# Dense products of a two-layer retention and RWKV-7 trunk: three products of 16-bit halves against one product of unsplit 32-bit floats

## The chip, the cores and the metric

The kernel runs on one core of one Trainium2 chip. The metric is the device time of one execution in microseconds (us). Engines are named as in the profile: PE is TensorE's matmul stream, PEld its weight loads, DVE is VectorE, ACT is ScalarE, POOL is GpSimd, SP is the queue from which the kernel issues its DMAs.

## The reference, cut to what matters

Two layers work on 1,024 latent tokens and 256 context tokens, 1,024 channels wide, all in 32-bit floats. Each layer normalises and modulates its input, sends it through one input projection, feeds two groups of heads (chunked retention, and an RWKV-7 delta-rule scan with a low-rank path for decay and learning rate), gates both, and adds an output projection to the residual:

```python
hl = rms_norm(xl, norm_w[layer]) * (1.0 + sc_l[:, None]) + sh_l[:, None]
pl = hl @ w_in[layer]                                   # 1024 -> 4*512 + 1664 + 512 columns
ql, kl, vl, gr_l, rw_l, gw_l = jnp.split(pl, IN_SPLITS, axis=-1)
...
w_log = -jax.nn.softplus(-(w0[d] + jnp.tanh(xw) @ w2[d])) - 0.5
a = jax.nn.sigmoid(a0[d] + xa @ a2[d])                  # the LoRA products
bonus = jnp.sum(hs(r) * hs(k) * r_k, axis=-1, keepdims=True) * hs(v)
```

The output projection is `mix @ w_out[layer]`, where mix holds the gated outputs of both groups (1,024 channels).

## The kernel before, in words

All 1,280 tokens (10 tiles of 128) lie along the free axis, channels on the partitions. A dense product has a 128x128 block of weights as its stationary operand and 256, 258 or 512 tokens as its moving operand; eight K tiles are summed in one PSUM bank.

**The dense products.** The helper `w_block` (L313) loads a column block of weights as 32-bit floats, two K tiles to a DMA, into `wraw` (3 buffers), and `w_split` (L308) makes two 16-bit halves of it: ACT writes the rounded half `whi` scaled by 16 (L309), ACT scales the raw block in place (L310), and POOL subtracts (L311) to give `wlo`. The normalised input is split likewise in `norm_chunk` (L332): `h_hi` by ACT, `h_lo` by DVE or POOL (L349 to L356). `project_steps` (L465) then issues three 16-bit products for each K tile, hi by hi, hi by lo and lo by hi (L477 to L479). The output projection does the same in `out_sum` (L799, products L804 to L806) with the halves of the mixed channels that `mix_in` (L785) makes. The LoRA stage `zstage` (L687) reads its input back from HBM twice over (tile `lap`), splits it and its weights, and multiplies in two 16-bit passes (L707). The sums over heads for the bonus (`head_sums`, L718) take two passes of the type float32r, of a rounded half and of its rest.

**The scan.** `prep` and `prep2` (L893, L934) prepare a step of 128 tokens in both directions, with a chain of small products, DVE masks and transposes and ACT copies; `seq` (L1031) carries the state through it. There are 40 steps in a layer, 10 for each of four pairs of heads. Their products are 32-bit and small (64 or 128 columns) or 16-bit (L980 to L1026).

**The order.** The dense work is a generator that yields its cost in units of microseconds; `pump` (L1199) draws from it a quota for each scan step (`QUOTA`, 15 in layer 0, 12 to 13 in layer 1), so that projections stand between the links of the scan on PE's queue. The scan is issued at high priority. When all dense work of a layer has been drawn, `out_last` (L852) adds the last two blocks of the output projection, normalises, and in the last layer writes the result. A projection yields `24 * (m1 - m0) / 2400`.

Of the kernel before, what the change touches and what calls it, by code (L numbers as in the profile page):

```python
# [11 lines left out]
F32R = mybir.dt.float32r  # L12
# [7 lines left out]
D = 1024  # L20
# [12 lines left out]
WS = 16.0  # L33
# [11 lines left out]
WB = 2  # L45
RAMP = 5.0
# [8 lines left out]
RB = 3  # L55
WMB = 3
XTB = 4
RETW = 32
NTM = (5, 7)
XB = 4  # L60
QUOTA = ((15.0, 15.0), (12.0, 13.0))
# [60 lines left out]
def hybrid_kernel(ctx: ExitStack, tc: tile.TileContext, a: dict, out: bass.AP, dbg: dict | None = None):  # L122
# [57 lines left out]
    bones32 = ln_pool.tile([128, 128], F32, name="bones32")  # L180
    load(bones32, a["c_bo"])
# [12 lines left out]
    bones = const.tile([128, 128], F32R, name="bones")  # L194
    nc.vector.tensor_copy(bones, bones32)
    bones2 = const.tile([128, 2], F32, name="bones2")
    nc.vector.tensor_copy(bones2, bones32[:, 0:128:64])
# [33 lines left out]
    la_d = dscr([2, 128, TOK], "la")  # L231
# [76 lines left out]
    def w_split(hi, lo, raw):  # L308
        nc.scalar.activation(hi, raw, AF.Copy, scale=WS)  # L309
        nc.scalar.activation(raw, raw, AF.Copy, scale=WS)  # L310
        nc.gpsimd.tensor_tensor(lo, raw, hi, ALU.subtract)  # L311

    def w_block(src, c0, rows=tuple(range(8))):  # L313
        halves = []
        for r0 in range(0, len(rows), 4):
            hi = wp.tile([128, 4, 128], F16, tag="whi", name="whi", bufs=WB)
            lo = wp.tile([128, 4, 128], F16, tag="wlo", name="wlo", bufs=WB)
            for q in range(r0, min(r0 + 4, len(rows)), 2):
                ks = slice(q - r0, q - r0 + 2)
                raw = wp.tile([128, 2, 128], F32, tag="wraw", name="wraw", bufs=RB)  # L320
                b0, b1 = rows[q:q + 2]
                cols = src[128 * b0:128 * b1 + 128, c0:c0 + 128].rearrange("(k p) n -> p k n", p=128)
                load(raw, cols[:, 0:b1 - b0 + 1:b1 - b0])
                w_split(hi[:, ks], lo[:, ks], raw)
            halves.append((hi, lo))
        return halves
# [5 lines left out]
    def norm_chunk(pool, l, h, mod, tiles, rs, get):  # L332
# [7 lines left out]
        for k in range(8):  # L340
            tm = pool.tile([128, 512], F32, tag="ntm", name="ntm", bufs=NTM[l])
            A, sh = mod["A"][:, c, k:k + 1], mod["B"][:, c, k:k + 1]
            by_pool = k % 4 == 1
            if by_pool:
                nc.gpsimd.tensor_tensor(tm[:, 0:n], get(k), rsb[:, 0:n], ALU.mult)
                nc.gpsimd.tensor_scalar(tm[:, 0:n], tm[:, 0:n], A, sh, ALU.mult, ALU.add)
            else:
                nc.vector.scalar_tensor_tensor(tm[:, 0:n], get(k), A, rsb[:, 0:n], ALU.mult, ALU.mult)
            for o, t0, m in _runs(tiles):  # L349
                hi, lo, t = h[0][:, k, t0:t0 + m], h[1][:, k, t0:t0 + m], tm[:, o:o + m]  # L350
                if by_pool:
                    nc.scalar.copy(hi, t)
                    nc.gpsimd.tensor_tensor(lo, t, hi, ALU.subtract)
# [11 lines left out]
    for l in range(DEPTH):  # L365
# [20 lines left out]
        nc.vector.tensor_scalar(hprm[:, 20:24], prm[:, R_RET:R_RET + 4], 0.5 / WS ** 2, None, ALU.mult)  # L386
# [32 lines left out]
        h = (hp.tile([128, 8, TOK], F16, name="h_hi"), hp.tile([128, 8, TOK], F16, name="h_lo"))  # L419
        h_hi, h_lo = h  # L420
# [44 lines left out]
        def project_steps(c0, pieces, sink):  # L465
            halves = w_block(w_in, c0)
            for piece in pieces:
# [4 lines left out]
                for hf in range(2):  # L472
                    hi, lo = halves[hf]
                    for k in range(4):
                        kk = 4 * hf + k
                        first, stop = kk == 0, kk == 7
                        nc.tensor.matmul(p[:, 0:n], hi[:, k, :], h_hi[:, kk, m0:m1], start=first, stop=False)  # L477
                        nc.tensor.matmul(p[:, 0:n], hi[:, k, :], h_lo[:, kk, m0:m1], start=False, stop=False)  # L478
                        nc.tensor.matmul(p[:, 0:n], lo[:, k, :], h_hi[:, kk, m0:m1], start=False, stop=stop)  # L479
                sink(p, m0, t0, t1)  # L480
                yield 24 * (m1 - m0) / 2400

        def conv(dst, p, m0, t0, t1, b):
# [5 lines left out]
            nc.scalar.activation(c[:, a0:a0 + w], p[:, o - 1 + a0:o - 1 + a0 + w], AF.Copy, scale=1.0 / WS)  # L489
# [28 lines left out]
        def ret_keys(rp, c):  # L518
# [3 lines left out]
            def sink(p, m0, t0, t1):  # L522
                nc.scalar.activation(kt[:, t0:t1], p[:, 0:t1 - t0], AF.Copy, scale=0.125 / WS)
                rope(kt[:, t0:t1], t0, t1)
# [3 lines left out]
        def ret_states(rp, c):  # L528
# [4 lines left out]
            def qsink(p, m0, t0, t1):  # L533
                nc.scalar.activation(qt[:, t0:t1], p[:, 0:t1 - t0], AF.Copy, scale=1.0 / WS)
                rope(qt[:, t0:t1], t0, t1)

            def vsink(p, m0, t0, t1):
                vch = [t256("vch") for _ in range(0, t1 - t0, 256)]
                for u, x in enumerate(vch):
                    nc.scalar.activation(x, p[:, 256 * u:256 * u + 256], AF.Copy, scale=1.0 / WS)  # L540
# [55 lines left out]
            yield from merge(own_states(), 4.3, queries(), 26)  # L596
# [69 lines left out]
        def gate_of(p):  # L666
            th = t256("gth")
            nc.scalar.activation(th, p[:, 0:256], AF.Tanh, scale=0.5 / WS)
# [4 lines left out]
        def lora():  # L673
            def sink(p, m0, t0, t1):
                la = t256("la")
                conv(la, p, m0, t0, t1, 12)
                nc.scalar.activation(la[0:64], la[0:64], AF.Tanh)
                for i in range(2):
                    for q in range(2):
                        load(la_d[i, 64 * q:64 * q + 64, t0:t1], la[64 * i:64 * i + 64])  # L680
# [6 lines left out]
        def zstage(p):  # L687

            raw = tz("wz")
            for i in range(2):  # L690
                src = a["rwkv_a2" if i else "rwkv_w2"][l][:, :, 128 * p:128 * p + 128].rearrange("d k n -> k d n")
                for q in range(2):
                    load(raw[64 * q:64 * q + 64, i].rearrange("k (d n) -> k d n", d=2), src)
            wz = pre.tile([128, 2, 256], F16, tag="wz", name="wz")
            nc.scalar.activation(wz, raw, AF.Copy, scale=WS)
            nc.vector.scalar_tensor_tensor(wz[64:128], raw[64:128], WS, wz[64:128], ALU.mult, ALU.subtract)
            for t0, t1, _, _ in CONV:
                la = tz("lap")
                load(la, la_d[:, :, t0:t1].rearrange("i p t -> p i t"))
                for i in range(2):  # L700
                    lh, ll = [pre.tile([128, 256], F16, tag="lr", name=nm, bufs=4) for nm in ("lh", "ll")]
                    nc.scalar.copy(lh, la[:, i])
                    nc.vector.tensor_tensor(ll, la[:, i], lh, ALU.subtract)
                    pz = pj("pz")
                    for d in range(2):
                        for q, lq in enumerate((lh, ll)):
                            nc.tensor.matmul(pz[:, 256 * d:256 * d + 256], wz[:, i, 128 * d:128 * d + 128], lq,  # L707
                                             start=(q == 0), stop=(q == 1))
                    th = tz("zth")
                    for d in range(2):  # L710
                        nc.scalar.activation(th[:, d], pz[:, 256 * d:256 * d + 256], AF.Tanh,
                                             bias=(ha0 if i else hw0)(d, p), scale=0.5 / WS)
# [4 lines left out]

        def head_sums(dst, x):  # L718

            xh, xl = [pre.tile([128, 256], F32R, tag="tr", name=nm, bufs=4) for nm in ("xh", "xlo")]  # L720
            nc.scalar.copy(xh, x)
            nc.gpsimd.tensor_tensor(xl, x, xh.bitcast(F32), ALU.subtract)
            nc.tensor.matmul(dst, bones, xh, start=True, stop=False)
            nc.tensor.matmul(dst, bones, xl, start=False, stop=True)

        def features(p):
# [29 lines left out]
            def vsink(pp, m0, t0, t1):  # L756
# [10 lines left out]
                head_sums(pp[:, 256:512], kt[:, t0:t1])  # L767
# [6 lines left out]
            yield from (rp if p else merge(zstage(p), 4.3, rp, 13))  # L774
# [10 lines left out]
        def mix_in(pool, tiles, b, key, bufs):  # L785
            n = 128 * len(tiles)
            mh = pool.tile([128, n], F16, tag=f"mh{key}", name="mh", bufs=bufs)
            ml = pool.tile([128, n], F16, tag=f"ml{key}", name="ml", bufs=bufs)
            for u in range(0, len(tiles), 2):
                raw = pre.tile([128, 2, 256], F32, tag="tz", name="mraw", bufs=TZB)[:, 0]  # L790
                for o, t0, m in _runs(tiles[u:u + 2]):
                    load(raw[:, o:o + m], mix_d[b][:, t0:t0 + m])
                piece = slice(128 * u, 128 * u + 256)
# [3 lines left out]
            return mh, ml  # L797

        def out_sum(x, tiles, k, parts):  # L799
# [3 lines left out]
            for i, ((hi, lo), (mh, ml)) in enumerate(parts):  # L803
                nc.tensor.matmul(p, hi, mh, start=(i == 0), stop=False)  # L804
                nc.tensor.matmul(p, hi, ml, start=False, stop=False)
                nc.tensor.matmul(p, lo, mh, start=False, stop=(i == len(parts) - 1))  # L806
            nc.vector.scalar_tensor_tensor(x, p, gmod[:, c, k:k + 1], x, ALU.mult, ALU.add)

        def out_part(chunks, key, stay):
# [6 lines left out]
            for k in range(8):  # L816
                halves = w_block(a["w_out"][l], 128 * k, EARLY)
                if stay:
                    out_last_weights(k)
                w = [[t[:, i % 4, :] for t in halves[i // 4]] for i in range(len(EARLY))]  # L820
                w += [[t[:, i, 128 * k:128 * k + 128] for t in ws] for i in range(len(LATE))]
                for tiles, ms in zip(chunks, mix):
# [10 lines left out]
                    yield 3 * len(ms) * 128 * len(tiles) / 2400  # L833
# [460 lines left out]
```

## Time and profile before

| | before |
|---|---|
| median of 3 runs | 2540.67 us (2540.04 to 2550.09) |
| the profiled execution | 2541.74 us |
| its span, first to last instruction | 2540.0 us |
| mean granted clock of PE in it | 0.945 of full speed |
| PE busy | 2332.3 us (92%) in 25223 instructions |
| DVE, ACT, POOL busy | 2016.9, 1209.1, 1017.3 us |
| moved by DMA | 302.82 MB, mean 119 GB/s |

Busy time counts every stretch in which an instruction of the engine is under way. Consecutive matmuls overlap in the records, since each record runs to the end of its drain; so the time from one start to the next, and not the duration, is what a product costs in a stream.

### The profile page before, as it was taken

How to read it: one execution, taken by the hardware profiler on the slowest of the kernel's cores; microseconds unless marked ns; L12 is line 12 of the kernel's file. 1: busy time of each engine (PE TensorE's matmuls, PEld its weight loads, DVE VectorE, ACT ScalarE, POOL GpSimd, SP SyncE). 2: the span in 40 equal slices, each digit the busy share in tenths (PEclk: the TensorE clock that was granted, in tenths of full speed). 3: DMA queues.
4: the chain of work that ended last, by engine and by line, in shares of the span. 5: the costliest groups of instructions: out<-in, count | busy, mean ns of one | idle time of the engine just before them, and what ended most of it. 6: DMA issues, size and time to landing. Idle time of an engine off the chain costs nothing. (4 is left out here: it accounts for less than half of the span.)

```text
span 2540.0 us, 68274 instructions
## 1 busy us (share of the span) xinstructions
PE 2332.3 (92%) x25223; PEld 1750.5 (69%) x25223; DVE 2016.9 (79%) x5822; ACT 1209.1 (48%) x3621; POOL 1017.3 (40%) x1511
## 2 busy tenths in 40 slices
PE   5789999999999999999986898999999999998997
PEld 2367767886787676777655677678768767676754
DVE  2658987998888787898657688889979988779866
ACT  4454554455455443345446545545645544334443
POOL 1444443344433433344425344444443444343442
PEclk8889999999999999799988899999999999987998
DMA  8754342444333432235433543434434433323444
GB/s 315 278 173 109 103 117 78 112 110 121 80 111 107 111 86 74 75 107 162 139 120 94 153 115 101 111 97 121 118 93 109 116 109 86 88 73 102 128 132 130
DMA packets 540013, 302.82 MB, mean 119 GB/s; under 512 B 239026, under 2 KB 526880, under 8 KB 537632
## 3 DMA queue, kind: packets, MB, share of 16 engines
q1 hardware_dynamic: 539680, 298.46, 41.0%
q8 instruction: 199, 3.26, 0.5%
q14 instruction: 134, 1.10, 0.1%
HBM read 212.21 MB, written 86.11 MB: 117 GB/s over the span
## 5 line engine op out<-in xcount | busy, mean ns | idle before, releaser
L477 PE MATMUL pproj<-h_hi,whi 128*128 128x256 f16 (+2 forms) x2128 | 632.2, 299 | 8.3 <-ACT h_hi L355 2.8
L478 PE MATMUL pproj<-h_lo,whi 128*128 128x256 f16 (+2 forms) x2128 | 632.3, 298 | 8.1 <-DVE h_lo L356 6.9
L479 PE MATMUL pproj<-h_hi,wlo 128*128 128x256 f16 (+2 forms) x2128 | 630.5, 298 | 4.5 <-POOL wlo L311 4.4
L311 POOL TENSOR_TENSOR wlo<-wraw,whi 128x256 f16<-128x256 f32 x360 | 252.2, 713 | 275.8 <-ACT wraw L310 230.9
L479 PEld LDWEIGHTS <-wlo 128*128 128x128 f16 x2128 | 214.0, 101 | 84.1 <-issue 13.1
L477 PEld LDWEIGHTS <-whi 128*128 128x128 f16 x2128 | 214.4, 101 | 74.3 <-issue 10.9
L478 PEld LDWEIGHTS <-whi 128*128 128x128 f16 x2128 | 213.3, 100 | 75.7 <-issue 16.1
L973 DVE STREAM_TRANSPOSE ttb<-tz 64x256 f16<-64x256 f16 x480 | 208.7, 435 | 29.2 <-ACT tz L994 24.4
L994 ACT CAST tz<-pinv 128x256 f16<-128x256 f32 x400 | 144.5, 370 | 178.1 <-PE pinv L993 161.6
L946 PE MATMUL pm<-own,bk 64*128 64x128 f32 (+1 forms) x1280 | 211.7, 300 | 9.5 <-DVE gq L949 4.6
L309 ACT ACTIVATE whi<-wraw 128x256 f16<-128x256 f32 x360 | 138.4, 412 | 153.9 <-DMA wraw<-in_w_in_dram 51.0
L963 POOL TENSOR_TENSOR il<-gq,c_id 64x256 f32<-64x256 f32 x160 | 122.9, 768 | 201.4 <-DVE gq L949 194.2
L946 PEld LDWEIGHTS pm<-own,bk 64*128 64x128 f32 x1280 | 168.9, 197 | 36.0 <-issue 10.9
L991 DVE TENSOR_TENSOR xx<-pinv,lvm 128x256 f16<-128x256 f32 x400 | 163.2, 416 | 36.0 <-PE pinv L980 32.7
L1049 PE MATMUL pseq<-st,own 64*64 64x64 f32 x2432 | 154.7, 231 | 0.0
L964 POOL TENSOR_TENSOR lo<-il,hi 64x256 f16<-64x256 f32 x160 | 116.9, 731 | 86.5 <-DVE hi L959 71.4
L310 ACT ACTIVATE wraw<-wraw 128x256 f32<-128x256 f32 x376 | 144.8, 410 | 4.4 <-ACT sbp L584 0.3
L980 PEld LDWEIGHTS <-hi 128*128 128x128 f16 x1920 | 105.1, 100 | 44.6 <-issue 17.3
L949 DVE TENSOR_TENSOR gq<-pm,c_m 128x256 f32<-128x256 f32 (+1 forms) x320 | 115.3, 400 | 25.0 <-PE pm L946 24.2
L1063 POOL TENSOR_TENSOR sf<-st,f 128x128 f32<-128x128 f32 x152 | 66.4, 437 | 164.7 <-DVE st L1081 147.9
L993 PE MATMUL pinv<-xx,ttb 128*128 128x64 f16 x1600 | 113.7, 196 | 16.6 <-DVE xx L991 15.4
L980 PE MATMUL pinv<-tz,hi 128*128 128x64 f16 x1600 | 115.6, 197 | 12.2 <-DVE tz L983 6.0
(250 smaller groups left out, 5648.9 us busy)
## 6 DMA issues: line engine op xcount, KB each, us to landing
ft<-feat SPq DMA_DIRECT2D x320, 160.0 KB
wraw<-in_w_in_dram SPq DMA_DIRECT2D x264, 128.0 KB
feat<-zth SPq DMA_DIRECT2D x80, 256.0 KB
wm<-in_w_mod_dram SPq DMA_DIRECT2D x16, 1024.0 KB
wraw<-in_w_out_dram SPq DMA_DIRECT2D x112, 128.0 KB
lap<-la SPq DMA_DIRECT2D x40, 256.0 KB
uv<-vt SPq DMA_DIRECT2D x320, 32.0 KB
wm<-in_w_mod_dram SPq DMA_DIRECT2D x16, 512.0 KB
```

What stands on the lines that cost most here:

```text
L309: nc.scalar.activation(hi, raw, AF.Copy, scale=WS)
L310: nc.scalar.activation(raw, raw, AF.Copy, scale=WS)
L311: nc.gpsimd.tensor_tensor(lo, raw, hi, ALU.subtract)
L477: nc.tensor.matmul(p[:, 0:n], hi[:, k, :], h_hi[:, kk, m0:m1], start=first, stop=False)
L478: nc.tensor.matmul(p[:, 0:n], hi[:, k, :], h_lo[:, kk, m0:m1], start=False, stop=False)
L479: nc.tensor.matmul(p[:, 0:n], lo[:, k, :], h_hi[:, kk, m0:m1], start=False, stop=stop)
L946: nc.tensor.matmul(pm[h][:, i, d, 0:q1], bk[HR[h], i, d, :], own[HR[h], i, d, 0:q1], start=True, stop=True)
L973: eng(idr(dst[HR[h], :, :, 64 * h:64 * h + 64]), idr(src[HR[h]]))
L980: nc.tensor.matmul(q[:, i, d, :], hi[:, i, d, :], id16 if n == 0 else tz[:, i, d, :], start=True, stop=True)
L991: nc.vector.tensor_tensor(xx, q, mk, ALU.mult)
L994: nc.scalar.copy(tzn, tp)
L1049: rm = nc.tensor.matmul(pq[HR[h], k, d, :], lhs, rhs, start=False, stop=stop, skip_group_check=True)
```

## The change

Every dense product takes its operands as 32-bit floats, one product for each K tile. `w_split`, the scale by 16 and its inverse, the 16-bit tiles and the splitting of the input, of the LoRA operands, of the head sums and of the mixed channels are gone. Weights are multiplied straight from the tile that the DMA fills (10 buffers in place of 3). The LoRA input stays in SBUF (`lora_t`), both halves of it stacked on the partitions, against weights padded with zeros (`lora_w`). All units of the generator that stand for dense products, and the quotas, are two thirds of what they were; the other units stay.

```diff
-RAMP = 5.0
+RAMP = 3.4
-RB = 3
+RB = 10
-RETW = 32
+RETW = 21
-QUOTA = ((15.0, 15.0), (12.0, 13.0))
+QUOTA = ((10.0, 10.0), (8.0, 8.7))
...
-    def w_split(hi, lo, raw):
-        nc.scalar.activation(hi, raw, AF.Copy, scale=WS)
-        nc.scalar.activation(raw, raw, AF.Copy, scale=WS)
-        nc.gpsimd.tensor_tensor(lo, raw, hi, ALU.subtract)
...
     def w_block(src, c0, rows=tuple(range(8))):
+        parts = []
+        for q in range(0, len(rows), 2):
+            raw = wp.tile([128, 2, 128], F32, tag="wraw", name="wraw", bufs=RB)
+            b0, b1 = rows[q:q + 2]
+            cols = src[128 * b0:128 * b1 + 128, c0:c0 + 128].rearrange("(k p) n -> p k n", p=128)
+            load(raw, cols[:, 0:b1 - b0 + 1:b1 - b0])
+            parts += [raw[:, 0, :], raw[:, 1, :]]
+        return parts
...
-                    nc.scalar.activation(hi, t, AF.Identity, bias=sh)
-                    nc.vector.scalar_tensor_tensor(lo, t, sh, hi, ALU.add, ALU.subtract)
+                    nc.scalar.activation(dst, t, AF.Identity, bias=sh)
...
-                        nc.tensor.matmul(p[:, 0:n], hi[:, k, :], h_hi[:, kk, m0:m1], start=first, stop=False)
-                        nc.tensor.matmul(p[:, 0:n], hi[:, k, :], h_lo[:, kk, m0:m1], start=False, stop=False)
-                        nc.tensor.matmul(p[:, 0:n], lo[:, k, :], h_hi[:, kk, m0:m1], start=False, stop=stop)
+                for k in range(8):
+                    nc.tensor.matmul(p[:, 0:n], parts[k], h[:, k, m0:m1], start=(k == 0), stop=(k == 7))
                 sink(p, m0, t0, t1)
-                yield 24 * (m1 - m0) / 2400
+                yield 16 * (m1 - m0) / 2400
...
-                        for q, lq in enumerate((lh, ll)):
-                            nc.tensor.matmul(pz[:, 256 * d:256 * d + 256], wz[:, i, 128 * d:128 * d + 128], lq,
-                                             start=(q == 0), stop=(q == 1))
+                        nc.tensor.matmul(pz[:, 256 * d:256 * d + 256], lora_w[:, i, d, :], lora_t[:, t0:t1], start=True, stop=True)
...
-                head_sums(pp[:, 256:512], kt[:, t0:t1])
+                nc.tensor.matmul(pp[:, 256:512], bones, kt[:, t0:t1], start=True, stop=True)
...
-                nc.scalar.copy(mh[:, piece], raw)
-                at["ml"] = at.get("ml", 0) + 1
-                (nc.gpsimd if at["ml"] % 3 == 0 else nc.vector).tensor_tensor(ml[:, piece], raw, mh[:, piece], ALU.subtract)
+            m = pool.tile([128, 128 * len(tiles)], F32, tag=f"mx{key}", name="mix", bufs=bufs)
+            for o, t0, n in _runs(tiles):
+                load(m[:, o:o + n], mix_d[b][:, t0:t0 + n])
...
-            for i, ((hi, lo), (mh, ml)) in enumerate(parts):
-                nc.tensor.matmul(p, hi, mh, start=(i == 0), stop=False)
-                nc.tensor.matmul(p, hi, ml, start=False, stop=False)
-                nc.tensor.matmul(p, lo, mh, start=False, stop=(i == len(parts) - 1))
+            for i, (w, m) in enumerate(parts):
+                nc.tensor.matmul(p, w, m, start=(i == 0), stop=(i == len(parts) - 1))
...
-                    yield 3 * len(ms) * 128 * len(tiles) / 2400
+                    yield 2 * len(ms) * 128 * len(tiles) / 2400
```

## Rows read from the trace of the kernel before

**Rows 1.** The page, first part: busy time, share of the span, instructions of each engine

```profile
PE 2332.3 (92%) x25223; PEld 1750.5 (69%) x25223; DVE 2016.9 (79%) x5822; ACT 1209.1 (48%) x3621; POOL 1017.3 (40%) x1511
```

**Rows 2.** Busy time by stretch: us, each engine's busy time, granted clock, DMA

```profile
17.00:140.00 123.00, 88.69 (x544) 40.85 (x544) 54.48 (x92) 50.14 (x116) 34.09 (x33) 0.83 0.83 300
600.00:1100.00 500.00, 485.49 (x5346) 369.34 (x5345) 414.08 (x1250) 221.69 (x680) 198.37 (x294) 0.96 0.35 94
1034.00:1071.00 37.00, 35.79 (x315) 29.98 (x316) 30.54 (x102) 14.27 (x44) 10.24 (x16) 0.50 0.28 68
1340.00:1700.00 360.00, 317.64 (x3320) 246.33 (x3318) 291.75 (x789) 189.06 (x555) 159.91 (x238) 0.92 0.40 111
2450.00:2540.00 90.00, 72.97 (x648) 44.23 (x648) 51.50 (x140) 35.20 (x102) 26.18 (x41) 0.90 0.40 121
```

**Rows 3.** PE's instructions by line and shape: busy us, mean ns, idle before

```profile
L477 PE MATMUL pproj<-h_hi,whi 128*128 128x256 f16 x912 | 254.2, 280 | 1.3 <-DVE gs L670 1.1
L477 PE MATMUL pproj<-h_hi,whi 128*128 128x258 f16 x832 | 232.9, 281 | 7.1 <-ACT h_hi L355 2.8 <-ACT craw L489 2.7 <-ACT zth L711 1.2
L477 PE MATMUL pproj<-h_hi,whi 128*128 128x512 f16 x384 | 146.8, 382 | 0.0
...
L804 PE MATMUL pout<-mh,whi 128*128 128x256 f16 x240 | 68.0, 286 | 3.3 <-ACT whi L309 2.5 <-DVE xo L807 0.2
...
L707 PE MATMUL pz<-lh,wz 128*128 128x256 f16 x160 | 42.1, 285 | 7.7 <-ACT craw L489 5.1 <-ACT lh L702 1.4 <-ACT zth L711 1.1
L271 PE MATMUL pmod<-wm,silu 128*2 128x512 f32 x192 | 37.6, 703 | 20.1 <-DMA wm<-in_w_mod_dram 20.1
L804 PE MATMUL pout<-mh,whi 128*128 128x512 f16 x96 | 37.2, 387 | 0.4 <-ACT whi L309 0.4
...
L804 PE MATMUL pout<-mh,wlh 128*128 128x256 f16 x56 | 15.8, 286 | 3.2 <-DVE x L807 2.5 <-ACT mh L794 0.3
...
L723 PE MATMUL pvt<-xh,bones 128*128 128x256 f32 x36 | 14.2, 394 | 0.5 <-ACT vs L763 0.5
...
L804 PE MATMUL pout<-mh,wlh 128*128 128x512 f16 x32 | 12.7, 403 | 2.0 <-ACT mh L794 1.2 <-ACT wlh L309 0.6
```

**Rows 4.** PE in order of time, two streams of 16-bit products: start us, us, instruction

```profile
69.21 0.27 PE L477 MATMUL pproj<-h_hi,whi 128*128 128x256 f16 x1
...
69.65 0.27 PE L478 MATMUL pproj<-h_lo,whi 128*128 128x256 f16 x1
...
600.24 0.38 PE L478 MATMUL pproj<-h_lo,whi 128*128 128x512 f16 x1
...
600.89 0.38 PE L478 MATMUL pproj<-h_lo,whi 128*128 128x512 f16 x1
```

**Rows 5.** PE in order of time: modulation products, by 110.30 us and to their end

```profile
110.18 0.61 PE L271 MATMUL pmod<-wm,silu 128*2 128x512 f32 x4
110.18 1.04 PE L271 MATMUL pmod<-wm,silu 128*2 128x512 f32 x8
```

**Rows 6.** PE in order of time: products with 128x128 weights of 32 bits

```profile
601.83 0.93 PE L946 MATMUL pm<-own,bk 64*128 64x128 f32 x6
...
603.46 0.38 PE L723 MATMUL pvt<-xh,bones 128*128 128x256 f32 x1
603.68 0.28 PE L724 MATMUL pvt<-xlo,bones 128*128 128x256 f32 x1
603.80 0.39 PE L479 MATMUL pproj<-h_hi,wlo 128*128 128x512 f16 x1
```

**Rows 7.** All engines by line: the dearest work of the splitting

```profile
L311 POOL TENSOR_TENSOR wlo<-wraw,whi 128x256 f16<-128x256 f32 x360 | 252.2, 713 | 275.8 <-ACT wraw L310 230.9 <-issue 9.7 <-PE pout L806 4.9
...
L309 ACT ACTIVATE whi<-wraw 128x256 f16<-128x256 f32 x360 | 138.4, 412 | 153.9 <-DMA wraw<-in_w_in_dram 51.0 <-PE pproj L478 43.9 <-DMA wraw<-in_w_out_dram 14.8
```

**Rows 8.** PE in order of time: first and last entry into dense products

```profile
64.83 0.27 PE L477 MATMUL pproj<-h_hi,whi 128*128 128x256 f16 x1
...
2524.60 0.27 PE L804 MATMUL pout<-mh,wlh 128*128 128x256 f16 x1
```

More of the change, by code (lines that the diff above doesn't have):

```diff
@@ L11 @@
 F32 = mybir.dt.float32
-F32R = mybir.dt.float32r
 F16 = mybir.dt.float16
@@ L44 @@
 LANES = 2
-WB = 2
-RAMP = 5.0
+RAMP = 3.4
 FTB = 1
@@ L305, in merge @@
             yield w
-    def w_split(hi, lo, raw):
-        nc.scalar.activation(hi, raw, AF.Copy, scale=WS)
-        nc.scalar.activation(raw, raw, AF.Copy, scale=WS)
-        nc.gpsimd.tensor_tensor(lo, raw, hi, ALU.subtract)
     def w_block(src, c0, rows=tuple(range(8))):
[L314 to L326, printed above, removed]
+        parts = []
[6 more added lines that the diff above has]
+        return parts
     sbp = []
@@ L385, in hybrid_kernel @@
         nc.vector.tensor_scalar(hprm[:, 0:20], prm[:, R_W0:R_W0 + 20], 0.5, None, ALU.mult)
-        nc.vector.tensor_scalar(hprm[:, 20:24], prm[:, R_RET:R_RET + 4], 0.5 / WS ** 2, None, ALU.mult)
+        nc.vector.tensor_scalar(hprm[:, 20:24], prm[:, R_RET:R_RET + 4], 0.5, None, ALU.mult)
         ka2 = lay.tile([128, 4], F32, tag="ka2", name="ka2")
@@ L465, in project_steps @@
         def project_steps(c0, pieces, sink):
-            halves = w_block(w_in, c0)
+            parts = w_block(w_in, c0)
             for piece in pieces:
@@ L594, in queries @@
                     yield from ret_gates(rp)
-            yield from merge(own_states(), 4.3, queries(), 26)
+            yield from merge(own_states(), 4.3, queries(), 17.4)
             for d in range(2):
@@ L674, in sink @@
             def sink(p, m0, t0, t1):
-                la = t256("la")
+                la = lora_t[:, t0:t1]
                 conv(la, p, m0, t0, t1, 12)
                 nc.scalar.activation(la[0:64], la[0:64], AF.Tanh)
-                for i in range(2):
-                    for q in range(2):
-                        load(la_d[i, 64 * q:64 * q + 64, t0:t1], la[64 * i:64 * i + 64])
             yield from project_steps(COL_LORA, CONV, sink)
@@ L716, in zstage @@
                 yield 0.86
[L718 to L724, printed above, removed]
         def features(p):
@@ L773, in features @@
             rp = project_steps(COL_RW + 128 * p, CONV[1:] if last else CONV, rsink)
-            yield from (rp if p else merge(zstage(p), 4.3, rp, 13))
+            yield from (rp if p else merge(zstage(p), 4.3, rp, 8.7))
             for w in project_steps(COL_RW + 1024 + 128 * p, CONV, vsink):
@@ L785, in mix_in @@
         def mix_in(pool, tiles, b, key, bufs):
[L786 to L793, printed above, removed]
-                nc.scalar.copy(mh[:, piece], raw)
-                at["ml"] = at.get("ml", 0) + 1
-                (nc.gpsimd if at["ml"] % 3 == 0 else nc.vector).tensor_tensor(ml[:, piece], raw, mh[:, piece], ALU.subtract)
-            return mh, ml
+            m = pool.tile([128, 128 * len(tiles)], F32, tag=f"mx{key}", name="mix", bufs=bufs)
+            for o, t0, n in _runs(tiles):
+                load(m[:, o:o + n], mix_d[b][:, t0:t0 + n])
+            return m
         def out_sum(x, tiles, k, parts):
@@ L816, in out_part @@
             for k in range(8):
-                halves = w_block(a["w_out"][l], 128 * k, EARLY)
+                w = w_block(a["w_out"][l], 128 * k, EARLY)
                 if stay:
                     out_last_weights(k)
-                w = [[t[:, i % 4, :] for t in halves[i // 4]] for i in range(len(EARLY))]
-                w += [[t[:, i, 128 * k:128 * k + 128] for t in ws] for i in range(len(LATE))]
+                w += [ws[0][:, i, 128 * k:128 * k + 128] for i in range(len(LATE))]
                 for tiles, ms in zip(chunks, mix):
@@ L832, in out_part @@
                             load(x_d[k][:, t0:t0 + m], x[:, o:o + m])
[L833 removed]
+                    yield 2 * len(ms) * 128 * len(tiles) / 2400
             close_pool(key)
         def out_last_weights(q):
[L837 removed]
             cols = a["w_out"][l][:, 128 * q:128 * q + 128].rearrange("(k p) n -> p k n", p=128)
[L839 to L840 removed]
+            load(ws[0][:, :, 128 * q:128 * q + 128], cols[:, LATE[0]:LATE[1] + 1:LATE[1] - LATE[0]])
         def x_in(pool, tiles):
@@ L860, in out_last @@
                 if parts:
-                    out_sum(x[:, k, :], tiles, k, [([t[:, i, 128 * k:128 * k + 128] for t in ws], m) for i, m in parts])
+                    out_sum(x[:, k, :], tiles, k, [(ws[0][:, i, 128 * k:128 * k + 128], m) for i, m in parts])
             if not last:
@@ L1153, in feats @@
             if p + 1 < NP:
-                yield from merge(zstage(p + 1), 4.3, features(p + 1), 44)
+                yield from merge(zstage(p + 1), 4.3, features(p + 1), 32)
                 ready.add(p + 1)
@@ L1164, in stream @@
                 thin = ret_out(p - 1, cs[p - 1], out_tiles[::2]) if p else ()
-                yield from merge(thin, 13, feats(p), 63 if p + 1 < NP else 26)
+                yield from merge(thin, 13, feats(p), 45 if p + 1 < NP else 17.4)
                 if p + 1 < NP:
@@ L1176, in first @@
                 ow = open_pool("ow", side)
-                ws[:] = [ow.tile([128, 2, D], dt, name=nm) for nm, dt in (("wlh", F16), ("wll", F16))]
+                ws[:] = [ow.tile([128, 2, D], F32, name="wlate")]
                 yield from out_part(out_order[cut:], "om0", False)
```

64 lines of the change are left out of this document (19 added, 45 removed).

## Prediction

> **What bounds the kernel now.** I read the page's first part first: PE is busy for 92% of the span and has the most to do; DVE comes next, at 79%, and ACT and POOL stay under half [rows 1]. The table by stretch shows that this is no average over unlike stages: in the middle of layer 0 PE is busy for 485 of 500 us, so there nearly every added microsecond of PE's work is a microsecond of time [rows 2]. It has gaps at the start (34 us, DMA at 0.83 of its engines), in layer 1 (42 of 360 us) and in the last 90 us (17) [rows 2]. All its idle time is 2540 - 2332 = 208 us [rows 1].
>
> A busy PE in these rows is not PE at its peak, so the next view is the order of time. Two records of a 256-column 16-bit product, four products apart, start 0.44 us apart, though each lasts 0.27; two of 512 columns, three apart, start 0.65 us apart [rows 4]. A product in a stream therefore costs 0.11 us (256) or 0.217 us (512): one column in each cycle of 2.4 GHz, and its weight load is hidden. The projections' line L477 stands three times, as L477, L478 and L479, with 912, 832 and 384 products of 256, 258 and 512 columns each [rows 3]. At those intervals the three lines take 3 x (1744 x 0.11 + 384 x 0.217) = 826 us, a third of the span.
>
> **What a product of 32-bit floats costs.** The kernel has some already. The modulation issues 96 of them (three calls, eight K tiles, four groups) and the profile counts 192 instructions at L271 [rows 3]: each product is two passes. How long is a pass of 512 columns? Eight instructions are four products that lie in four different column groups of the array. Four of them have started by 110.30 us and end, together, at 110.18 + 0.61; all eight end at 110.18 + 1.04 [rows 5]. So the second passes run 0.43 us behind the first, and 512 columns in 0.43 us are two cycles for each column. Two passes make four cycles a column: 0.43 us for 256 columns, 0.86 us for 512.
>
> The bound on the other side is another row. The head sums run in float32r, 256 columns with weights of 32 bits, and from the second of them to the next instruction there are 0.12 us [rows 6], one cycle a column. If a pass of plain 32-bit floats ran like that, a product would cost 0.24 us against three times 0.11. I take 0.43: L271 is the same type as the new products and more than 256 columns wide, while float32r is a different type and takes one instruction where plain floats take two. The other end stays as a rival.
>
> The Trainium skill, page "FP8 and Floating Point Precision", section "TensorE Precision Notes", says that true FP32 takes four passes through the array (high and low halves, each by each), which speaks against the change: three products of halves are one pass fewer. By that page a 256-column product would be, as an estimate, four times the 16-bit one, 0.44 us; L271 agrees [rows 5].
>
> **The change part by part.**
>
> *Projections.* 256 and 258 columns: from 0.33 to 0.43 us, +0.10 x 1744 = +174. 512 columns: from 0.65 to 0.86, +0.21 x 384 = +81. Together +255 us.
>
> *Output projection.* The rows show 240 and 56 products of 256 columns and 96 and 32 of 512 for each of its three lines; 24 more of 256 columns take the last block straight from the scan. (320 x 0.10) + (128 x 0.21) = +59 us [rows 3].
>
> *LoRA.* 160 products go from two passes, 0.22 us, to one product at 0.43: +34 us [rows 3]. *Head sums*: 36 products from 0.34 (0.22 + 0.12 [rows 6]) to 0.43: +3 us.
>
> So far +351 us, all of it on PE.
>
> *Weight loads.* In a stream a pass of 128 columns with 128 columns of 32-bit weights costs at most about 0.13 us: six records in 0.93 us, of which the last one's 0.27 is its own length [rows 6]. A load is then no longer than that, and hides behind a pass of 0.215. But the first of a group is not hidden: from L723 to L724 there are 0.22 us, from L724 on 0.12, so the entry costs 0.10 more, while the 16-bit L479 that follows at 603.80 is entered without such a gap [rows 6]. The scan cuts the dense work into pieces: in order of time PE enters it 907 times, from the first to the last entry shown [rows 8]. 907 x 0.10 = +91 us if each entry pays, nothing if the load is fetched ahead. I take it in full, since the only row with such an entry pays.
>
> *What is given back.* Gone are POOL's 252 us for `wlo`, ACT's 138 us for `whi` with its second scaling pass, and smaller splits on DVE and POOL [rows 7]. None of these engines bounds a stretch, so I cost this at nothing by itself; what hides it is PE's queue. It helps only through PE's idle time. If all stretches came to the 3% idle of 600 to 1100 us, then outside the start and the end 157 us of idle would become about 70. More dense work per link of the scan also covers more of each wait. I take -65; bounds 0 and -145.
>
> *The clock.* The mean granted clock of PE was 0.945 (the front table), so throttling lost about 0.055 x 2540 = 140 us. The stretch from 1034 to 1071 us shows where: PE is busy for 35.8 of 37 us, at half clock, 1.2 GHz [rows 2], in small products of the scan and the retention output. What keeps the clock up between 600 and 1100, at 0.96, is the share of dense products. Their time grows by a third, so I give back a third: -45; bounds 0 and -140, with the loss as a rival.
>
> The Trainium skill, page "TensorE: Matmul & The Clock Gate", section "Why this matters for your kernels", says that continuous work on TensorE releases the throttle. By that the busier PE would win back all 140 us and the sum would end near 2795. The row at half clock with PE busy throughout does not agree, so the row decides.
>
> *Loads, buffers and pacing.* Weights come by the same DMAs into 10 buffers instead of 3, so a block waits for DMA no longer than before; the round trip of the LoRA input through HBM is gone. The quotas and the units of dense work both shrink to two thirds, but the LoRA, retention and state units stay, so each quota now holds less dense work. Adding up the yields by the code: layer 1 before, 490 units against 490 of quotas and 20 of ramp, the last unit drawn in step 38 of 40; after, 357 against 327 and 14, so some 30 us of PE's work is left when the scan ends. Then `out_last` for all eight latent tiles waits on PE's queue behind it, where before the first tiles were finished during the last steps. The tail has PE at 73 of 90 us [rows 2]; I add +15, bounds 0 and +30.
>
> **Sum.** +351 + 91 - 65 - 45 + 15 = +347. From the span, 2540.0 + 347 = 2887; the profiled execution stood 1.7 us above its span and 1.1 above the median, so some 2,890 us, 14% slower. Extremes of the terms give 2,696 (no entry cost, -145, -50 on the clock) and 3,012 (351 + 91 + 30).
>
> **The rivals.**
>
> *PE has room.* Busy PE includes drains (0.27 recorded, 0.11 taken), and many links of the scan wait for one result while nothing streams. If half of the 351 fell into such holes and entries were hidden, the time would be 2540 + 175 = about 2,715. For it: the gaps of layer 1. Against it: in 600 to 1100 us the starts follow each other and only 15 of 500 us are idle. Chance 0.10.
>
> *The clock falls.* If the 32-bit products hold the clock less well than the 16-bit ones, as in the half-clock stretch that is mostly 32-bit work, and the mean goes from 0.945 to 0.85, then 2890 x 0.945 / 0.85 = about 3,210. Against it: those are products on parts of the array, and the new ones fill it. Chance 0.07.
>
> *A pass takes one cycle a column.* The place is each dense product; the price is 0.24 us in place of 0.33, and 0.43 in place of 0.65. Then 2064 x -0.09 + 512 x -0.22 = -298, LoRA +3, entries +91: -204, and the kernel would be faster, about 2,340 with POOL and ACT relieved. It decides if a pass of 256 columns stays under about 0.14 us, entries included. For it: L724's 0.12. Against it: L271's 0.43. Chance 0.07.
>
> *Nothing measurable*, gains and losses level: 0.02.
>
> **How the numbers follow.** My forecast has 0.74. The time is its sum. Range 2,700 to 3,020: it holds nearly all of the forecast's cases and most of the first rival's, and leaves out the two far ones; a low end further down would buy little. Half a per cent, about 13 us, is what a measurement of this kernel can tell from no change. Faster by more: 0.07 (the cheap pass). Within: 0.02. Slower: 0.91.
>
> **What would show it right or wrong.** PE's row at the projection line should have 4256 instructions (two for each of 2128 products), starts 0.215 us apart within a 256-column stream and 0.43 for 512; an entry should cost 0.1 us more. PE's share should rise to 94% or more, ACT's and POOL's busy time fall by 250 us or more each, with no gain in time. The gaps of layer 1 should shrink, the granted clock rise a little. Starts 0.11 us apart would make the forecast wrong at its root; a clock below 0.9, or PE's idle time above 250 us, would make it too low; a PE under 90% busy at a time below 2,750 would mean that the holes took the work.

## The result, and the profile after

The changed kernel takes 2888.27 us (median of 4 runs, 2887.52 to 2890.42) against 2540.36 us for the kernel before beside it: a ratio of 1.1366, 95% interval 1.1331 to 1.1401. The time is the forecast one; several terms of its sum are not.

The page of the changed kernel, first part (busy time, share, instructions), as in [rows 1]:

```profile
PE 2758.2 (96%) x22647; PEld 2050.1 (71%) x22647; DVE 1899.1 (66%) x5630; ACT 916.8 (32%) x2655; POOL 697.9 (24%) x1063
```

ACT lost 292 us and POOL 319, and the time rose all the same. PE has fewer instructions and 426 us more of busy time; its idle time is 2886.4 - 2758.2 = 128 us, after 208.

The granted clock, from the view of the cores:

```profile
core 0: 2886.4 us, clock 0.938
```

PE by line and shape, the rows that answer to [rows 3]:

```profile
L455 PE MATMUL pproj<-h,wraw 128*128 128x256 f32 x1824 | 452.3, 392 | 0.2 <-DVE gs L646 0.2
L455 PE MATMUL pproj<-h,wraw 128*128 128x258 f32 x1664 | 418.5, 397 | 2.9 <-ACT h L339 1.5 <-ACT zth L672 0.9 <-ACT craw L465 0.5
L455 PE MATMUL pproj<-h,wraw 128*128 128x512 f32 x768 | 354.3, 602 | 0.0
...
L669 PE MATMUL pz<-lora_t,lora_w 128*128 128x256 f32 x320 | 92.6, 413 | 4.7 <-ACT zth L672 2.6 <-ACT craw L465 2.0
```

The counts are exactly two for each product: 1824 for 912, 1664 for 832, 768 for 384, 320 for the 160 of LoRA. PE in order of time gives the price of a pass, as [rows 4] gave that of a 16-bit product (start us, us, instruction):

```profile
703.47 4.05 PE L455 MATMUL pproj<-h,wraw 128*128 128x256 f32 x18
...
2736.15 5.31 PE L749 MATMUL pout<-mix,wraw 128*128 128x512 f32 x12
```

Eighteen passes of 256 columns take 4.05 us, of which the last one's length is 0.38: (4.05 - 0.38) / 17 = 0.216 us. Twelve of 512 columns take 5.31 with 0.60 at the end: 4.71 / 11 = 0.428. Both are two cycles of 2.4 GHz for each column, and two passes make the four that were read from the modulation [rows 5].

The table by stretch, columns as in [rows 2]:

```profile
17.00:140.00 123.00, 103.38 (x500) 55.70 (x494) 40.47 (x76) 42.79 (x94) 21.29 (x18) 0.83 0.83 297
600.00:1100.00 500.00, 499.61 (x4086) 365.90 (x4086) 332.66 (x1011) 156.59 (x470) 120.27 (x180) 1.00 0.30 82
1114.00:1195.00 81.00, 73.64 (x694) 62.19 (x695) 63.98 (x200) 23.80 (x74) 24.25 (x37) 0.56 0.21 52
1500.00:1800.00 300.00, 278.16 (x2077) 223.98 (x2076) 190.82 (x505) 119.59 (x334) 85.39 (x133) 0.94 0.33 93
2507.00:2565.00 58.00, 56.58 (x488) 47.92 (x488) 45.03 (x151) 19.16 (x56) 16.84 (x26) 0.50 0.22 56
2800.00:2886.00 86.00, 62.83 (x584) 45.91 (x583) 55.67 (x164) 21.45 (x64) 11.03 (x18) 0.74 0.22 74
```

In the middle of layer 0 PE is busy for 499.6 of 500 us at full clock: the products go back to back and there is no hole left. In layer 1, from 1500 to 1800 us, its idle share is 22 of 300 us, where the gappy stretch before had 42 of 360 [rows 2]. Two stretches are the opposite. From 2507 to 2565 us PE is busy for 56.6 of 58 us and runs at half clock, 1.2 GHz; from 1114 to 1195 it is at 0.56. In both almost no dense product runs. The dearest groups of PE between 2507 and 2565 us:

```profile
L596 PE MATMUL pss<-qt,kt 64*128 64x128 f32 x24 | 7.6, 463 | 0.0
L989 PE MATMUL pseq<-st,own 64*64 64x64 f32 x72 | 6.8, 322 | 0.0
L599 PE MATMUL pss<-sbp,qt 64*128 64x128 f32 x24 | 6.3, 417 | 0.0
```

They use 64 rows of the array, some of them 64 of its columns too.

**Where the 346 us are.** For every product on PE I took the time from its start to the next start, and split it into what its columns need at 2.4 GHz (one cycle a column for 16 bits, two for a pass of 32, and 2.5 ns) and the rest. "Dense" are projections, output and LoRA; an entry is a dense product behind one of the scan or retention. The head sums, which are no part of "dense" here, ran in float32r before and are taken there at the one cycle that their rows show [rows 6]. Sums in us:

| | before | after | difference | in the prediction |
|---|---|---|---|---|
| dense, what the columns need | 1044.5 | 1402.3 | +357.8 | +348 |
| dense, rest at 954 and 694 entries | 15.3 | 54.3 | +39.0 | +91 |
| dense, rest elsewhere | 140.8 | 65.2 | -75.6 | |
| scan and others, columns | 1055.8 | 1063.5 | +7.7 | +3 (head sums) |
| scan and others, rest | 273.1 | 289.3 | +16.2 | |
| the two rests outside entries | 413.9 | 354.5 | -59.4 | -65 - 45 + 15 = -95 |

The first five lines are +345 together, beside 346.4 us between the spans. The rests hold waits, switches and the clock: passes of 256 columns that lie in a half-clock stretch start 0.427 us apart, after 0.216 at full clock (medians). Some products of the scan and the modulation start 7 ns apart, side by side in parts of the array, and count with all their columns here, so of the two lines on "scan and others" only the differences mean something.

### The profile page after: what moved, and what is told of

Same layout as the page of the kernel before. It is cut to its first block, busy times and chain, and to the rows that moved or that the text cites. A ratio compares the mean times of both kernels' runs of the same rounds, so it can differ in the third digit from the quotient of the medians.

```text
span 2886.4 us, 61009 instructions
## 1 busy us (share of the span) xinstructions
PE 2758.2 (96%) x22647; PEld 2050.1 (71%) x22647; DVE 1899.1 (66%) x5630; ACT 916.8 (32%) x2655; POOL 697.9 (24%) x1063
## 5 line engine op out<-in xcount | busy, mean ns | idle before, releaser
L455 PE MATMUL pproj<-h,wraw 128*128 128x258 f32 (+2 forms) x4256 | 1217.3, 432 | 3.1 <-ACT h L339 1.5
L455 PEld LDWEIGHTS pproj<-h,wraw 128*128 128x128 f32 x4256 | 787.3, 194 | 253.7 <-issue 150.2
L749 PE MATMUL pout<-mix,wraw 128*128 128x256 f32 (+1 forms) x672 | 218.9, 463 | 1.3 <-DMA mix<-mix 1.3
L989 PE MATMUL pseq<-st,own 64*64 64x64 f32 x2432 | 164.8, 239 | 0.0
L749 PEld LDWEIGHTS pout<-mix,wraw 128*128 128x128 f32 x672 | 123.3, 196 | 49.7 <-issue 34.6
L989 PEld LDWEIGHTS pseq<-st,own 64*64 64x64 f32 x2432 | 117.5, 145 | 17.3 <-issue 0.3
L933 PEld LDWEIGHTS <-ttb 128*128 128x128 f16 x1600 | 85.5, 101 | 50.1 <-issue 18.6
L871 POOL TENSOR_TENSOR own<-ft,ep 128x256 f32<-128x256 f32 x72 | 54.7, 760 | 271.4 <-PE pseq L989 257.1
L848 DVE TENSOR_TENSOR_SCAN cs<-ones,ft 128x64 f32<-128x64 f32 x160 | 49.3, 308 | 92.2 <-DMA ft<-feat 91.4
L465 ACT COPY craw<-pproj 128x258 f32<-128x258 f32 (+2 forms) x126 | 46.8, 372 | 197.2 <-PE pproj L455 140.1
```

Of the source, the lines that this page charges most:

```text
L455: nc.tensor.matmul(p[:, 0:n], parts[k], h[:, k, m0:m1], start=(k == 0), stop=(k == 7))
L749: nc.tensor.matmul(p, w, m, start=(i == 0), stop=(i == len(parts) - 1))
L933: nc.tensor.matmul(tp[:, i, d, :], ttb[:, i, d, :], xx[:, i, d, :], start=True, stop=True)
L989: rm = nc.tensor.matmul(pq[HR[h], k, d, :], lhs, rhs, start=False, stop=stop, skip_group_check=True)
```

## The experiments

**Six and ten of eight.** The straight test of "time follows the passes": take a quarter of the projections' passes away (the last two K tiles are left out of each sum), and add a quarter.

```diff
-                for k in range(8):
-                    nc.tensor.matmul(p[:, 0:n], parts[k], h[:, k, m0:m1], start=(k == 0), stop=(k == 7))
+                for k in range(6):
+                    nc.tensor.matmul(p[:, 0:n], parts[k], h[:, k, m0:m1], start=(k == 0), stop=(k == 5))
```

> The changed kernel, but each projection multiplies six of its eight K tiles (the last two are left out of the sum; their weights are still loaded). Theory (TensorE's passes set the time, two cycles a column and two passes): the projections' streams, 1744 x 0.43 + 384 x 0.86 = 1080 us, lose a quarter, 270 us; with somewhat more waiting the time is 2,620 to 2,690 us. Rival (loading the unsplit weights or the new pacing sets it): the same loads and the same order, so 2,850 to 2,890. Rival (the clock): the granted clock drops below 0.92 since fewer dense columns run, and the time stays above 2,700.

```diff
+                for k in (0, 1):
+                    nc.tensor.matmul(p[:, 0:n], parts[k], h[:, k, m0:m1], start=(k == 0), stop=(k == 1))
                 for k in range(8):
```

> The changed kernel with ten products for eight K tiles in each projection: the first two are multiplied once more ahead of the sum, whose first product then clears the bank, so that the result is as before. Adds a quarter of 1080 us, 270 us, of dense passes. Six of eight took off 270 us of passes and gave only 188 us, at a clock of 0.907 after 0.938. Theory A (time follows the passes one for one while TensorE is full): 2,888 + 270 = 3,140 to 3,165, clock near 0.94. Theory B (dense work also holds the clock up, so each added microsecond returns some): clock 0.95 or more and 3,080 to 3,135.

Six took 2700.39 us (span 2698.6, granted clock 0.907), ten 3112.5 (3110.7, 0.961), each in a single execution. The first part of the page with six, and then with ten:

```profile
PE 2517.2 (93%) x21583; PEld 1887.9 (70%) x21583; DVE 1883.1 (70%) x5630; ACT 910.2 (34%) x2655; POOL 696.8 (26%) x1063
```

```profile
PE 3012.6 (97%) x23711; PEld 2229.0 (72%) x23711; DVE 1912.8 (61%) x5630; ACT 922.8 (30%) x2655; POOL 697.8 (22%) x1063
```

A change of 270 us of passes moved the time by 188 and by 224 us. The passes set the time, so the rival of loads and pacing falls; but not one for one. Six came out 10 us above the upper end of its theory and, by less than a microsecond, within the third condition, that of the clock; ten met its theory B. The clock rises with dense work, 0.907, 0.938, 0.961, and what throttling loses, (1 - clock) x span, is 251, 179 and 121 us (an upper figure, since PE's waits at half clock are counted in it). Subtract these differences from 270: 198 and 212, near the 188 and 224 that were measured. This is an accounting from one execution each, and no test by itself.

**Float32r, once, twice, and in the output too.** Same bytes and 32-bit weights, half the instructions at about one cycle a column. The weights get 3 buffers and their copies 8, in place of 10:

```diff
-        h = hp.tile([128, 8, TOK], F32, name="h")
+        h = hp.tile([128, 8, TOK], F32R, name="h")
...
+            if f32r:
+                wr = wp.tile([128, 2, 128], F32R, tag="wr", name="wr", bufs=8)
+                nc.scalar.copy(wr, raw)
+                raw = wr
             parts += [raw[:, 0, :], raw[:, 1, :]]
```

> The changed kernel with the projections alone in float32r, a 32-bit type that is rounded when it is written: the weights are written to it by one ACT copy, the input by the instruction that made it before. Products are less exact. Same bytes, same weight loads of 32 bits, one instruction in place of two. Theory (passes): starts 0.11 us apart for 256 columns, so the projections take 1744 x 0.112 + 384 x 0.217 = 279 us in place of 1080; TensorE no longer bounds the kernel, and the chain of the scan and DVE, 1899 us busy, do: 2,100 to 2,350 us. Rival (reading 4-byte operands or loading 32-bit weights is what costs): starts still 0.2 us apart or more, time above 2,550.

It took 2366.74 us in a single execution, 17 above the upper end. The granted clock was 0.842 over a span of 2364.9 us. The page's first part:

```profile
PE 2091.5 (88%) x20519; PEld 1658.1 (70%) x20519; DVE 1861.9 (79%) x5630; ACT 979.9 (41%) x2919; POOL 696.5 (29%) x1063
```

A row of PE by line and shape:

```profile
L460 PE MATMUL pproj<-h,wr 128*128 128x256 f32 x912 | 160.3, 318 | 10.1 <-DVE gs L651 5.0 <-ACT craw L470 4.0 <-ACT zth L677 0.9
```

And two streams in PE's order of time:

```profile
157.02 1.22 PE L460 MATMUL pproj<-h,wr 128*128 128x256 f32 x8 [0.48 <-ACT craw L470]
...
449.31 2.10 PE L460 MATMUL pproj<-h,wr 128*128 128x512 f32 x8
```

One instruction for each product now, x912 for the x1824 of plain floats. If the first start of a stream costs 0.1 us more and the last record lasts some 0.28 and 0.38, the steps are (1.22 - 0.38) / 7 = 0.12 us for 256 columns and (2.10 - 0.48) / 7 = 0.23 for 512; the medians over the whole trace are 0.119 and 0.232. So neither reading 4 bytes nor loading 32-bit weights costs the 0.43 us of a plain product; the two passes of two cycles do. The other side of the bound in the prediction, L724's 0.12 [rows 6], is real too, but belongs to float32r alone. Some 1080 - (1744 x 0.12 + 384 x 0.23) = 780 us of passes gave 521 us of time: throttling lost 0.158 x 2365 = 374 us in place of 179, and PE's idle time rose from 128 to 273.

The same with each sum computed twice:

```diff
-                for k in range(8):
+                for k in list(range(8)) * 2:
```

> Projections in float32r, each sum computed twice in a row into the same bank (the second start clears it, so the result is that of the single one): adds 279 us of passes at full clock. Theory (dense work holds the clock up, and TensorE has holes at 2366.7 us): the half-clock time falls from 750 us to 450 or less and the time rises by only 40 to 150 us, 2,405 to 2,515. Rival (time follows the passes): 2,640 us.

2462.49 us in a single execution, clock 0.910: 96 us more for some 298 us of passes by the steps above (279 in the expectation). The half-clock time, added up over the trace's clock records, is 442 us after 748, and PE's idle time is 181 us after 273. The rival falls; how the rest divides between clock and holes was not separated.

And the output projection in float32r as well (its weights and the mixed channels that come from HBM copied to that type by ACT):

```diff
-            m = pool.tile([128, 128 * len(tiles)], F32, tag=f"mx{key}", name="mix", bufs=bufs)
+            m = pool.tile([128, 128 * len(tiles)], F32R, tag=f"mx{key}", name="mix", bufs=bufs)
...
+                nc.scalar.copy(m[:, 128 * u:128 * u + 256], raw)
```

> Projections and output projection in float32r, one instruction of one cycle a column (less exact), each operand written to that type by one ACT copy; LoRA and head sums stay 32-bit floats. Projections alone came to 2366.7 us at a clock of 0.842, with TensorE busy 88%. The output's products go from 320 x 0.43 + 128 x 0.86 = 248 us to some 63. Theory (TensorE no longer bounds and the clock takes back part): 2,230 to 2,330 us, clock 0.80 to 0.84. Rival (the output part is still bound by TensorE and gives its 185 us in full): 2,180 or less.

2262.86 us (4 runs, 2246.43 to 2277.24), a ratio of 0.8902 to the kernel before, 0.8863 to 0.8940: faster than both kernels of this study, at a clock of 0.811 in the profiled execution. What the rounding to this type costs in exactness, no run here shows. The page's first part, with DVE now the nearest to PE:

```profile
PE 1948.5 (87%) x20071; PEld 1586.9 (71%) x20071; DVE 1849.9 (82%) x5630; ACT 1046.3 (47%) x3103; POOL 699.9 (31%) x1063
```

**The pacing.** All units and quotas back to the numbers of before, and then units at the four cycles that a column takes:

```diff
-RAMP = 3.4
+RAMP = 5.0
...
-QUOTA = ((10.0, 10.0), (8.0, 8.7))
+QUOTA = ((15.0, 15.0), (12.0, 13.0))
...
-                yield 16 * (m1 - m0) / 2400
+                yield 24 * (m1 - m0) / 2400
```

> The changed kernel with every unit and quota of the generator of dense work put back to the numbers of before. Theory (the products cost the time, the pacing only orders it): within 25 us of the changed kernel, 2,865 to 2,910 us; the work left at the scan's end gone, worth some 15 us. Rival (the smaller quotas starve the scan's steps and leave a tail): 2,840 us or less.

```diff
-QUOTA = ((10.0, 10.0), (8.0, 8.7))
+QUOTA = ((18.0, 18.0), (16.0, 16.5))
...
-                yield 16 * (m1 - m0) / 2400
+                yield 32 * (m1 - m0) / 2400
...
-                yield 0.86
+                yield 1.7
```

> The changed kernel with the generator's units for dense work set to four cycles a column, which is what the traces show, the LoRA unit to 1.7, and quotas and merges raised to match, so that dense products are spread over the scan's steps by their true length. Theory (the order is worth little, the passes cost the time): 2,870 to 2,900 us. Rival (the stretches at half clock without dense products come from the pacing): the granted clock rises above 0.95 and the time falls to 2,850 or less.

The old numbers took 2903.69 us, a ratio of 1.1407 (1.1373 to 1.1441); the true ones 2874.97, 1.1271 (1.1238 to 1.1305). The interval of the first overlaps the changed kernel's; that of the second lies below it, and its ratio is 0.8% lower. So putting the old quotas back gained nothing, and the tail that I had priced at +15 from the smaller ones was not shown: the numbers that leave no work at the scan's end are no faster. Spreading the dense work by its true length may be worth some 0.8%; from what, was not separated. The rival on the clock was not met either, 0.941 after 0.938.

**Is the relief of ACT and POOL worth anything?** The splitting of the weights put back into tiles that nobody reads, with 6 weight buffers for room, and its control:

```diff
-RB = 10
+RB = 6
...
+            hi, lo, t = [wp.tile([128, 2, 128], dt, tag=nm, name=nm, bufs=2) for nm, dt in (("shi", F16), ("slo", F16), ("st", F32))]
+            nc.scalar.activation(hi, raw, AF.Copy, scale=16.0)
+            nc.scalar.activation(t, raw, AF.Copy, scale=16.0)
+            nc.gpsimd.tensor_tensor(lo, t, hi, ALU.subtract)
```

> The changed kernel with the splitting of the weights done as before, two ACT passes and one POOL subtraction for each pair of K tiles, into tiles that nobody reads; the weights' buffers are 6 in place of 10 to make room. Theory (ACT and POOL bound nothing, and DMA's lead is ample): within 15 us of the changed kernel, 2,880 to 2,905. Rival (the relief of ACT and POOL shortens the scan's waits, which is how the LoRA part alone came out 10 us faster in spite of 34 us more passes): 2,915 us or more.

> The control of the splitting left in place: the changed kernel with 6 weight buffers in place of 10 and nothing else. Splitting with 6 buffers took 2911.6 us, the changed kernel 2888.3. Theory (the extra 23 us are the splitting's own, on ACT and POOL in the scan's way): 2,883 to 2,897. Rival (they come from fewer buffers, that is from late weights): 2,900 to 2,915.

Splitting with 6 buffers took 2911.59 us, ratio 1.1427 (1.1386 to 1.1469), between its two bands, so that the control decides; 6 buffers alone 2904.36, 1.1409 (1.1374 to 1.1444). The splitting adds 7 us, which the intervals do not separate from nothing: the 138 + 252 us of ACT and POOL at L309 and L311 [rows 7], and the second ACT pass, were hidden as work of these engines. Nothing waits for the halves here, so what a product's wait for them cost before is not tested. The 16 us between 10 and 6 buffers went the rival's way, though the two intervals overlap, so that fewer buffers cost time is likely and not shown.

**LoRA.** The LoRA part alone on the kernel before, and then its relief without its passes:

```diff
-                        for q, lq in enumerate((lh, ll)):
-                            nc.tensor.matmul(pz[:, 256 * d:256 * d + 256], wz[:, i, 128 * d:128 * d + 128], lq,
-                                             start=(q == 0), stop=(q == 1))
+                        nc.tensor.matmul(pz[:, 256 * d:256 * d + 256], lora_w[:, i, d, :], lora_t[:, t0:t1], start=True, stop=True)
```

> The kernel before with only the LoRA part of the change: input kept in SBUF, unsplit, one 32-bit product in place of two 16-bit passes. Theory (passes on TensorE count, relief elsewhere doesn't): 160 products x 0.21 us = 34 us slower, 2,560 to 2,580. Rival (what ACT, DVE and the DMA lose is worth more: 80 ACT casts, 80 DVE subtractions and 40 loads of 256 KB): 2,540 or faster.

```diff
+    lres = [const.tile([128, 2, TOK], F16, name=nm) for nm in ("lh", "ll")]
...
-                    lh, ll = [pre.tile([128, 256], F16, tag="lr", name=nm, bufs=4) for nm in ("lh", "ll")]
-                    nc.scalar.copy(lh, la[:, i])
-                    nc.vector.tensor_tensor(ll, la[:, i], lh, ALU.subtract)
+                    lh, ll = [t[:, i, t0:t1] for t in lres]
```

> The kernel before, with the LoRA input loaded and split into its two 16-bit halves once in a layer and kept, in place of once for each of the four pairs of heads; the products stay two 16-bit passes. This has three quarters of the relief that the unsplit LoRA had (60 of 80 ACT casts and DVE subtractions, 30 of 40 loads) and none of its 34 us of added passes. Theory (the LoRA part alone paid its 34 us and had 45 us back from relief): 2,495 to 2,520. Rival (its 34 us of passes fell into holes of TensorE's queue, and relief is worth nothing): 2,530 to 2,545.

Alone it is not 34 us slower but faster by a ratio of 0.9957 (0.9930 to 0.9983), 2535.14 us; the theory fell. The next guess, that relief had paid for it, fell too: three quarters of the relief without the passes give 0.9992 (0.9975 to 1.0009), 2545.75 us beside 2547.23. In the trace of the LoRA part alone the clock is 0.953 over 2529.4 us. The page's first part:

```profile
PE 2356.3 (93%) x25223; PEld 1776.9 (70%) x25223; DVE 1990.7 (79%) x5734; ACT 1182.0 (47%) x3533; POOL 1015.9 (40%) x1512
```

The gappy stretch of layer 1 in the table by stretch:

```profile
1340.00:1700.00 360.00, 321.80 (x3416) 251.06 (x3415) 283.75 (x773) 178.83 (x517) 155.56 (x230) 0.94 0.35 98
```

PE's idle time is 173 us after 208, and throttling loses 0.047 x 2529 = 119 us in place of 140: 35 and 21 us, together more than the 34 of the passes. Over all executions of this run the clock is 0.942 to 0.957, beside 0.937 to 0.945 in the kernel before. In the kernel before there was room for these few passes, in holes and in the clock. The rival *PE has room* is right for 34 us and wrong for 351. Which instructions filled which holes I did not separate.

## Why the prediction was right, point by point

**The cost of a product: right, and shown.** 0.432 and 0.857 us against 0.43 and 0.86. The count of two instructions, the steps in the streams and the two float32r kernels all say the same. The Trainium skill, page "FP8 and Floating Point Precision", section "TensorE Precision Notes", has the four passes; this kernel issues them as two instructions of two cycles a column. The sum of projections, output and LoRA, +348, measured +358; three products of 256 columns were taken at 0.33, where the steps of the whole trace are 0.109 each. The head sums, +3, measured +7.7 in columns, since the 0.34 of before had an entry in it.

**PE as the bound: right in the large.** The 270 us steps both ways move the time by 70% and 83%. The relief at nothing: right for the weights' splitting as work of ACT and POOL: put back, it was not told from nothing.

**The entries: too dear.** 91 us forecast, +39 measured. The 907 entries of before are counted without LoRA, 954 with it; after the change they are 647 and 694, so fewer entries pay. Why they are fewer was not tested. An entry costs 0.084 us in the median, where 0.10 was read from one pair of head sums [rows 6].

**The idle time: near.** 208 to 128 us, -80 for -65.

**The clock: the wrong sign.** I gave back 45 us for a third more dense time. The granted clock fell from 0.945 to 0.938, and what throttling loses rose from 140 to 179 us. The step that failed was to spread the gain evenly. In the middle of layer 0 the clock did rise, 0.96 to 1.00 from 600 to 1100 us. I added up the half-clock time under each product, from its start to the next start: 94 us under dense products before and 86 after, but 180 us under the others before and 269 after. So the rival that 32-bit products hold the clock less well is not what these traces show; the loss lies where no dense product runs. The longest stretches from one dense start to the next grew from 48, 30 and 22 us to 92, 66 and 42, and the half-clock rows, 1034 us before [rows 2], 1114 and 2507 us after, lie almost wholly in them. Why the order of work leaves them so long was not settled; the old numbers (81, 63 and 52 us) and the true units (78, 63 and 62) did not remove them. PE's records at 2507 us show it busy for 56.6 of 58 us at half clock. In the rule of the Trainium skill, page "TensorE: Matmul & The Clock Gate", section "Why this matters for your kernels", continuous work releases the throttle; those 56.6 busy microseconds of 58 speak against it once more.

**The tail: not shown, and not of the kind forecast.** The forecast left some 30 us of dense work over when the scan ends. In the trace the dense work runs out first: from 2787 to 2829 us PE has products of the scan and no dense one, and the last products of the output start behind it. The old numbers have such a stretch too, of 52 us. The last 86 us have PE idle for 23, where 90 us before had 17 [rows 2]; no experiment put that on the quotas.

So the forecast of +347 owes its closeness to errors that cancel, which is luck. In the table's accounting the entries are 52 too high, the passes with the head sums 14 too low, and idle time, clock and tail together give back 36 too much. The range has a slip as well: its low end takes -50 for the clock, where the bound given for that term is -140; with -140 it would be about 2,606. What carries the forecast is the one term of 358 us, and with that alone the time would have been forecast at about 2,900.

## What to carry to other kernels

Before an operand type is changed, find one product of that type in the old trace that is wide enough for its passes, not its weight load, to set the steps, and count its instructions: here a modulation matmul of 512 columns held the whole answer. Then ask what else the type could be: float32r costs little more than a quarter of plain floats (0.12 us after 0.43 for 256 columns) and, if its rounding is good enough for the use, beat both kernels. And do not price added or removed matmuls one for one: 270 us of dense ones moved the time by 188 and 224, with the clock rising as they were added.

## What was unexpected of the hardware

The clock did not follow PE's busy share: 92% stands at 0.945 in the kernel before, 93% at 0.907 with six of eight, and 56.6 busy us of 58 at half clock. With the same scan and a growing share of dense products the granted clock went 0.811, 0.842, 0.907, 0.938, 0.961 (float32r in projections and output, in projections alone, six, eight and ten K tiles of plain floats), and the float32r kernel lost more than twice as much to the throttle as the changed one, 374 after 179 us. But the amount of dense work is not the whole of it either. From start to next start, dense products take 1,201 us of the kernel before, at 0.945, and 1,242 us of six of eight, at 0.907. What differs is where they stand: the longest stretches from one dense start to the next are 48, 30 and 22 us before, and 105, 101 and 67 with six of eight. In each of these five traces the longest stretch at half clock has at most 5 us of dense products in it. That the spread of the dense work sets the clock is argued from this; no run changed the spread alone by much.
